# Order of work on VectorE and ScalarE at the end of layer 0 of a two-layer decoder trunk

## The chip, the cores and the metric

The kernel runs on one core of a Trainium2 chip. The metric is the device time of one execution in microseconds (us), the median of three runs. The engines are named as in the profile: PE is TensorE (matmuls; PEld its weight loads), DVE is VectorE, ACT is ScalarE, POOL is GpSimd, and SP issues the loads of weights. Each engine works through its own list of instructions in order; semaphores tie the lists together.

## What is computed

Two layers over 256 tokens of width 1024. Layer 0 mixes tokens by multi-head latent attention, layer 1 by causal attention in blocks with a relative bias from a table; each is followed by an MLP with squared ReLU. Cut to what matters here:

```python
def sq_relu_mlp(h, w_in, w_out):
    a = jax.nn.relu(h @ w_in)
    return (a * a) @ w_out

for i in range(DEPTH):                     # DEPTH = 2
    h = rms_norm(x, attn_norm[i])
    if i % 2 == 0:
        x = x + mla_mixer(h, ...)
    else:
        qkv = (h @ w_qkv).reshape(B, S, 3, 8, 128)
        q, k = rms_norm(qkv[:, :, 0], q_norm), rms_norm(qkv[:, :, 1], k_norm)
        ...                                # logits + table[t5_bucket(pos_q - pos_k)], causal, softmax, @ v, @ w_o
    h = rms_norm(x, mlp_norm[i])
    x = x + sq_relu_mlp(h, w_in, w_out)
```

All of it is float32.

## The kernel before

**Layout.** x is held transposed, as eight column tiles `x[:, d]` of 128 features by 256 tokens. A normed input h is not divided by its root mean square where it is made: h is x times the gain, and the factor of each token (`scale`, or `r3` in layer 1) is applied to the product.

**Three matmuls for one.** To keep float32 accuracy every operand is split in a high part, rounded to fp32r, and a low part, the rest. A product takes three matmuls (`mm3`): high x high, low x high, high x low. For h the parts are hTh (made on ACT) and hTl (made on DVE from x and hTh). For weights they are wh (a cast on ACT, L169) and wl (a subtraction on DVE, L178).

**Weights.** All weights are a list of units of 128x1024 (512 KB). SP loads a unit into one of four `raw` buffers, `hi` casts it, `lo` subtracts, and both results stand in rings of seven. The load of a unit can start when the `lo` of the unit four places ahead of it is done, since that frees its buffer. `hi` goes no further than seven units beyond the last that PE is done with. `both()` issues one `hi` and one `lo`; `fill()` issues `lo` and then `hi`; both do nothing where the ring is full. In what follows **w0, w1, w2 ...** are the units of `w_qkv` in layer 1, in the order in which PE needs them: w0 to w3 for the projection k0, w4 to w7 for q0, w8 to w11 for v0.

**The end of layer 0.** The second matmul of the MLP goes over the eight column tiles d = 0 to 7, in two rounds r; in the last round (r = 1) tile d is finished on the other engines, one after the other:

- `both()` in the middle of the tile's matmuls and `both()` at its end (in d = 6 these split w2 and w3, in d = 7 w4 and w5);
- what `run_fillers` has for this place: in d = 1, 3, 5 and 7 six additions of 0.3 us each that put a block of the relative bias into SBUF (`BiasBlock.add`, L1034); for d = 6 there is nothing;
- `t`: the product times `scale` (DVE, L976);
- `finish0`: x = t + x (L1041; on POOL, for d = 7 on DVE), hTh on ACT (L609), `fill()`, hTl on DVE (L611); for odd d also the square of two tiles of x on ACT (L299), which POOL adds to the sum of squares (L301; after the last tile L306).

The order of all this is the order in which the code issues it (`manual_schedule`); nothing is moved by a scheduler.

**The start of layer 1.** PE goes on with k0 at once: for each column k = 0 to 7 it needs hTh and hTl of that column as the stationary operand and wh and wl of unit w(k // 2) as the moving one; two token tiles of three matmuls each. Then comes q0 for the first token tile (24 matmuls, column k with unit w(4 + k // 2)), four small matmuls for the token sums, q0 for the second token tile, and the transposes of the normed k0 (L372). The norm of k0 is made of squares on ACT (L342), sums over them on DVE (L343), the token sums that DVE copies from PSUM (L316), roots on POOL (L270) and products on DVE (L352).

Of the kernel before, what the change touches and what calls it, by code (L numbers as in the profile page):

```python
# [25 lines left out]
KD = D // P  # L26
# [26 lines left out]
NR = 2  # L53
NPAIR = DFF // (2 * P * NR)
# [6 lines left out]
def trunk(ctx: ExitStack, tc: tile.TileContext, A, out):  # L61
# [9 lines left out]
    def ps():  # L71
        return psum.tile([P, 512], F32, name="ps", tag="ps")

    def room(pool, name):
        if ROOM[name]:
            pool.tile([P, ROOM[name] // 4], F32, name="room_" + name)

    def t2(*shape):
        return work.tile([P, *shape], F32, name="t2", tag="t2")

    def f32(ap):
        return ap.bitcast(F32)
# [4 lines left out]
    def mm3(o, a, b, start, stop, wide=None, between=None):  # L87

        for i, (w, t) in enumerate(((0, 0), (1, 0), (0, 1))):
            if wide and i == 0:  # L90
                mm(wide[0], a[w], wide[1], start, False)
            else:
                mm(o, a[w], b[t], start and i == 0, stop and i == 2)
            if between and between[0] == i:
                between[1]()
# [7 lines left out]
    def wider(bank, b):  # L103
        moved[0] = True
        return bank[:, :S + 2], flat(b[:, :2])[:, :S + 2]
# [55 lines left out]
    def hi(n=1, eng=nc.scalar):  # L161

        for _ in range(n):
            i = len(his)
            if i < min(used[0] + RING, len(units)):
                load_raw()
                w = units[i][1]
                his.append(wsp.tile([P, 1024], F32R, name="wh", tag="wh"))
                (eng.copy if eng is nc.scalar else eng.tensor_copy)(his[i][:, :w], raws[i][:, :w])  # L169

    def lo(n=1, eng=nc.vector):

        for _ in range(n):
            i = len(los)
            if i < len(his):
                w = units[i][1]
                los.append(wsp.tile([P, 1024], F32R, name="wl", tag="wl"))
                eng.tensor_sub(los[i][:, :w], raws[i][:, :w], f32(his[i][:, :w]))  # L178
                load_raw()

    def fill(n=1):
        lo(n)
        hi(n)

    def both(n=1):

        for _ in range(n):
            hi()
            lo()

    def unit(i):
        while len(his) <= i:
            hi()
        while len(los) <= i:
            lo()
        return his[i], los[i]

    def done(i):

        used[0] = max(used[0], i + 1)  # L200

    def part(u, sl):
        return u[0][:, sl], u[1][:, sl]
# [59 lines left out]
    def gain(name, i=0):  # L263
        return gains[:, GOFF[name][0] + i:GOFF[name][0] + i + 1]
# [18 lines left out]
    def hT(k, sl=slice(None)):  # L283
        return hTh[:, k, sl], hTl[:, k, sl]
# [323 lines left out]
    def make_h_filled(k, gname):  # L608
        nc.scalar.activation(hTh[:, k], x[:, k], AF.Copy, scale=gain(gname, k))  # L609
        fill()  # L610
        nc.vector.scalar_tensor_tensor(hTl[:, k], x[:, k], gain(gname, k), f32(hTh[:, k]),  # L611
                                       op0=OP.mult, op1=OP.subtract)
# [267 lines left out]
    for i in range(2):  # L880
        r = slice(i * PE_D, (i + 1) * PE_D)
# [16 lines left out]
    def mlp(l, base, fillers, inside, finish):  # L898

        with tc.tile_pool(name=f"mlp{l}", bufs=1) as pool:  # L900
            scale = pool.tile([P, S], F32, name="scale")
            room(pool, f"a{l}")
            a = [pool.tile([P, 2 * NPAIR, S], F32R, name=f"a{i}") for i in range(2)]
            sums = SumSquares()

            def run_fillers(r, j):
                for g in fillers:
                    if g[0] == (r, j):
                        g[1]()

            def first(b, r, j, split_k, between=None):
                u = [unit(b + 2 * j + i) for i in range(2)]
                p = [ps() for _ in range(2 if split_k else 1)]
                o = [p[f][:, :S] if split_k else p[0][:, f * S:(f + 1) * S] for f in range(2)]
                for f, k in [(f, k) for k in range(KD) for f in range(2)] if split_k else \
                        [(f, k) for f in range(2) for k in range(KD)]:
                    c = (k % 4) * 256 + f * P
                    wide = None
                    if k == f == 0 and not moved[0]:
                        wide = wider(p[f], hTh)  # L920
                    mm3(o[f], part(u[k // 4], slice(c, c + P)), hT(k), k == 0, k == KD - 1, wide,
                        between if (f, k) == (1, KD - 2) else None)
                done(b + 2 * j + 1)


                beside = not split_k and j < NPAIR - 1
                for f, n in ((0, 1), (1, 1)) if split_k else ((0, 2),):
                    src = o[f] if split_k else p[0]
                    rl = t2(n * S)
                    nc.scalar.activation(rl, src, AF.Relu)  # L930
                    sq = t2(n * S)
                    nc.vector.scalar_tensor_tensor(sq, src, 0.0, rl, op0=OP.max, op1=OP.mult)  # L932
                    if l == 1 and r == NR - 1:
                        sq3 = sq.rearrange("p (a b) -> p a b", b=S)
                        nc.vector.tensor_mul(sq3, sq3, scale[:, None, :].to_broadcast([P, n, S]))
                    if beside:
                        both()
                    ah, al = (i[:, 2 * j + f:2 * j + f + n].rearrange("p a b -> p (a b)") for i in a)
                    nc.scalar.copy(ah, sq)
                    nc.vector.tensor_sub(al, sq, f32(ah))  # L940
                both((1 if beside else 2) + (1 <= j < 4))
                run_fillers(r, j)

            for r in range(NR):
                b = base + r * (2 * NPAIR + 2 * KD)
                for j in range(NPAIR):
                    between = inside.get((r, j))
                    if r == 0 and j == 6:
                        pb = ps()
                        between = other_type(1, lambda: mm(pb[:, :S], ones, s, True, True))  # L950
                    first(b, r, j, r == 0 and j == 0, between)
                    if r == 0 and 1 <= j < 5:
                        sums.add(j - 1)
                    if r == 0 and j == 5:
                        s = sums.total()
                    if r == 0 and j == NPAIR - 1:
                        nc.vector.tensor_scalar(scale, pb[:, :S], 1.0 / D, EPS, op0=OP.mult, op1=OP.add)
                        nc.vector.reciprocal(scale, scale)
                b += 2 * NPAIR
                for d in range(KD):  # L960
                    bank = ps()
                    o = bank[:, :S]
                    for f in range(2 * NPAIR):
                        u = unit(b + 2 * d + f // 8)
                        c = (f % 8) * P
                        mm3(o, part(u, slice(c, c + P)), (a[0][:, f], a[1][:, f]), f == 0, f == 2 * NPAIR - 1,
                            wider(bank, a[0]) if f == 0 and not moved[0] else None,
                            inside.get((r, NPAIR + d)) if f == 2 * NPAIR - 2 else None)
                        if f == 7:
                            both()  # L970
                            done(b + 2 * d)
                    both()
                    run_fillers(r, NPAIR + d)
                    if l == 0 or r < NR - 1:
                        y = t2(S)
                        nc.vector.tensor_tensor(y, o, scale, op=OP.mult)  # L976
                        if r < NR - 1:
                            nc.gpsimd.tensor_add(x[:, d], y, x[:, d])  # L978
                            o = None
                        else:  # L980
                            o = y
                    if o is not None:
                        finish(d, o)
                    done(b + 2 * d + 1)


# [52 lines left out]
    def finish0(d, o):  # L1039
        eng = nc.vector if d == KD - 1 else nc.gpsimd  # L1040
        eng.tensor_add(x[:, d], o, x[:, d])  # L1041
        make_h_filled(d, "attn1")
        if d == 0:
            sums1[0] = SumSquares()
        if d % 2:
            sums1[0].add(d // 2)
# [167 lines left out]
```

## Time and profile before

| | |
|---|---|
| three runs | 564.36, 564.68, 564.85 us (median 564.68) |
| the profiled execution, its own time | 564.54 us |
| its span, first to last instruction | 562.7 us |
| granted TensorE clock, mean over the span | 0.997 |
| DMA queues of the weights | 54% of the 16 engines' span |

The page gives the busy time of each engine over the span, then groups of instructions: line, engine, operation, the tile written and the tiles read, count, busy time, mean length. A line such as L85 is that of a helper (`mm`), so PE's work is told apart by the names of the tiles. An answer in order of time has start, length (both in us), engine, line, operation, tiles and, in brackets, how long the engine was idle before and what ended it. Matmuls overlap: each is given 0.39 us at 512 columns though one starts every 0.23 us. A table by stretches gives, for each engine, busy time and number of instructions, and at the end the clock that TensorE was granted (1.00 is full speed), the share of the DMA engines and GB/s.

### The profile page before, as it was taken

Reading aid. Unit: us, or ns where it says so; the run is one execution under the profiler, and the core shown is the slowest. Engines: PE = TensorE matmul, PEld = TensorE weight load, DVE = VectorE, ACT = ScalarE, POOL = GpSimd, SP = SyncE. Lnnn points to the kernel's source line nnn. Section 1 sums busy time; section 2 is a strip of 40 time slices with the busy share of each in tenths; the row PEclk is TensorE's granted clock in tenths of the full one; section 3 lists DMA queues with packets and bytes.
Section 4 is the critical chain, followed back from the end, with each engine's and each line's share of the span. In section 5 each row is a group of like instructions: output and inputs, shape, how many; then the busy total and the mean of one; then the engine's idle time right before and its main releaser. Section 6 shows DMA issues by size and latency. Waiting matters only on the chain.

```text
span 562.7 us, 10806 instructions
## 1 busy us (share of the span) xinstructions
PE 554.5 (99%) x4346; PEld 527.3 (94%) x4346; DVE 396.4 (70%) x654; ACT 302.8 (54%) x495; POOL 94.6 (17%) x105
## 2 busy tenths in 40 slices
PE   8999999999999999999989999999999999999997
PEld 6878999999999999999868888999999999999997
DVE  5997777778987598766678466676876753877630
ACT  6989675665433356343455556646765332655420
POOL 4892100040232000011124100000130211000100
PEclk9999999999999999999989999999999999999999
DMA  8833444686675366544454553453775764575810
GB/s 299 296 123 118 146 139 158 187 280 190 188 223 189 112 217 196 176 155 157 152 182 123 186 191 115 147 181 113 230 224 181 251 201 150 159 219 185 265 45 29
DMA packets 29186, 99.57 MB, mean 177 GB/s; under 512 B 3824, under 2 KB 4720, under 8 KB 29136
## 3 DMA queue, kind: packets, MB, share of 16 engines
q1 hardware_dynamic: 28656, 97.94, 54.1%
q0 software_dynamic: 336, 0.92, 0.4%
q8 instruction: 34, 0.56, 0.4%
q14 instruction: 16, 0.13, 0.1%
q10 hardware_dynamic: 144, 0.02, 0.0%
HBM read 97.82 MB, written 1.05 MB: 176 GB/s over the span
## 4 chain that ended last, share of the span: by engine, by line
PE 95%; DVE 2%; DMA 1%; SPq 1%; issue 1%; POOL 0%; ACT 0%; DVEq 0%
PE ps L85 92%; PE ps L372 1%; PE ps L596 1%; DMA rowp<-in_rowp 1%; DVE wl L178 1%; SPq L158 0%; SPq L230 0%; DVE bias L1034 0%; POOL ang L393 0%; DVE hTl L280 0%; PE ps L512 0%; ACT wh L169 0%; POOL posf L391 0%; ACT hTh L609 0%; DVE x L1041 0%
## 5 line engine op out<-in xcount | busy, mean ns | idle before, releaser
L178 DVE TENSOR_TENSOR wl<-raw,wh 128x1024 fp32r<-128x1024 f32 x177 | 217.0, 1241 | 37.6 <-ACT wh L169 37.0
L169 ACT CAST wh<-raw 128x1024 fp32r<-128x1024 f32 x177 | 182.7, 1047 | 72.2 <-PE ps L85 53.6
L85 PE MATMUL ps<-a,wh 128*128 128x256 f32 x1024 | 175.3, 276 | 0.0
L85 PEld LDWEIGHTS ps<-a,wh 128*128 128x128 f32 x1024 | 154.4, 188 | 0.0
L85 PE MATMUL ps<-a,wl 128*128 128x256 f32 x512 | 142.1, 277 | 0.0
L85 PE MATMUL ps<-hTl,wh 128*128 128x256 f32 x512 | 141.7, 277 | 0.0
L85 PE MATMUL ps<-hTh,wl 128*128 128x256 f32 x512 | 141.7, 277 | 0.0
L85 PE MATMUL ps<-hTh,wh 128*128 128x256 f32 x512 | 141.3, 276 | 0.0
L85 PEld LDWEIGHTS ps<-hTl,wh 128*128 128x128 f32 x512 | 96.1, 188 | 0.1
L85 PEld LDWEIGHTS ps<-hTh,wh 128*128 128x128 f32 x512 | 96.1, 188 | 0.1
L85 PEld LDWEIGHTS ps<-a,wl 128*128 128x128 f32 x512 | 96.1, 188 | 0.0
L85 PEld LDWEIGHTS ps<-hTh,wl 128*128 128x128 f32 x512 | 96.1, 188 | 0.0
L930 ACT ACTIVATE t<-ps 128x512 f32<-128x512 f32 (+1 forms) x34 | 19.5, 572 | 67.5 <-PE ps L85 67.5
L85 PE MATMUL ps<-wh,hTh 128*128 128x512 f32 (+2 forms) x128 | 46.9, 392 | 3.7 <-ACT hTh L609 2.4
L85 PE MATMUL ps<-aT,wh 128*128 128x256 f32 (+1 forms) x256 | 50.4, 288 | 0.0
L932 DVE SCALAR_TENSOR_TENSOR t<-ps,t 128x512 f32<-128x512 f32 (+1 forms) x34 | 22.4, 659 | 38.4 <-ACT t L930 38.0
L85 PE MATMUL ps<-wl,hTh 128*128 128x512 f32 (+2 forms) x128 | 45.9, 384 | 0.2 <-DVE wl L178 0.2
L85 PE MATMUL ps<-wh,hTl 128*128 128x512 f32 (+2 forms) x128 | 45.7, 383 | 0.0
L85 PEld LDWEIGHTS ps<-aT,wh 128*128 128x128 f32 x256 | 40.3, 188 | 0.2
L609 ACT ACTIVATE hTh<-x,gains 128x256 fp32r<-128x256 f32 x24 | 12.2, 510 | 47.9 <-POOL x L1041 29.7
L85 PE MATMUL ps<-aT,wl 128*128 128x256 f32 x128 | 35.6, 278 | 0.0
L978 POOL TENSOR_TENSOR x<-t,x 128x256 f32<-128x256 f32 x16 | 19.4, 1211 | 93.4 <-DVE t L976 93.4
(166 smaller groups left out, 634.7 us busy)
## 6 DMA issues: line engine op xcount, KB each, us to landing
raw<-in_w_in_mlp SPq DMA_DIRECT2D x64, 512.0 KB, 4.1
raw<-in_w_out_mlp SPq DMA_DIRECT2D x64, 512.0 KB, 4.3
raw<-in_w_qkv SPq DMA_DIRECT2D x24, 512.0 KB, 4.2
raw<-in_w_u SPq DMA_DIRECT2D x8, 512.0 KB, 5.9
win<-in_w_in SPq DMA_DIRECT2D x8, 352.0 KB, 5.3
raw<-in_w_o0a SPq DMA_DIRECT2D x4, 512.0 KB, 3.6
raw<-in_w_o0b SPq DMA_DIRECT2D x4, 512.0 KB, 3.6
raw<-in_w_o1a SPq DMA_DIRECT2D x4, 512.0 KB, 3.8
```

The lines of the kernel that those rows point to most:

```text
L85: nc.tensor.matmul(o, a, b, start=start, stop=stop)
L169: (eng.copy if eng is nc.scalar else eng.tensor_copy)(his[i][:, :w], raws[i][:, :w])
L178: eng.tensor_sub(los[i][:, :w], raws[i][:, :w], f32(his[i][:, :w]))
L372: nc.tensor.transpose(pt[:, i * P:(i + 1) * P], yf[:, i * P:(i + 1) * P], ident)
L596: nc.tensor.transpose(pt[:, i * P:(i + 1) * P], self.p[:, i * P:(i + 1) * P], ident)
L609: nc.scalar.activation(hTh[:, k], x[:, k], AF.Copy, scale=gain(gname, k))
L930: nc.scalar.activation(rl, src, AF.Relu)
L932: nc.vector.scalar_tensor_tensor(sq, src, 0.0, rl, op0=OP.max, op1=OP.mult)
L978: nc.gpsimd.tensor_add(x[:, d], y, x[:, d])
```

## The change

In layer 0's last round, for d = 6 and d = 7, the second `both()` and `run_fillers` are issued behind `t` and `finish0` and not ahead of them. For these two tiles `finish0` makes h with `make_h` (L279 and L280 after the change), which issues hTh and hTl with no `fill()` in between; a `fill()` stands behind the moved `both()` instead. All other tiles, rounds and layer 1's MLP are as they were.

```diff
@@ in mlp(), the loop over the column tiles d @@
                         if f == 7:
                             both()
                             done(b + 2 * d)
-                    both()
-                    run_fillers(r, NPAIR + d)
+
+                    last = l == 0 and r == NR - 1 and d >= KD - 2
+                    if not last:
+                        both()
+                        run_fillers(r, NPAIR + d)
                     if l == 0 or r < NR - 1:
                         y = t2(S)
                         nc.vector.tensor_tensor(y, o, scale, op=OP.mult)
...
                     if o is not None:
                         finish(d, o)
+                    if last:
+                        both()
+                        fill()
+                        run_fillers(r, NPAIR + d)
                     done(b + 2 * d + 1)
@@ finish0 @@
         eng = nc.vector if d == KD - 1 else nc.gpsimd
         eng.tensor_add(x[:, d], o, x[:, d])
-        make_h_filled(d, "attn1")
+        (make_h_filled if d < KD - 2 else make_h)(d, "attn1")
```

Lines behind the edit move by three in `mlp` and by seven below it: L976 becomes L979, L1034 becomes L1041, L1041 becomes L1048.

DVE's list before, from the split of w3 (wl_3613) to hTl of column 7. The splits of w4 and w5 are wl_3649 and wl_3689; the two t are those of columns 6 and 7:

```order
L178 TENSOR_TENSOR wl_3613<-raw_3462,wh_3611 128x1024
L976 TENSOR_TENSOR t2_3617<-ps_3556,scale_1319 128x256
L611 SCALAR_TENSOR_TENSOR hTl_155<-x_81,gains_82,hTh_154 128x256
L178 TENSOR_TENSOR wl_3649<-raw_3500,wh_3647 128x1024
L178 TENSOR_TENSOR wl_3689<-raw_3540,wh_3687 128x1024
L1034 TENSOR_TENSOR bias_1312<-ps_3672,mask_146 128x8x16
L1034 TENSOR_TENSOR bias_1312<-ps_3672,bias_1312 128x8x16 x2
L1034 TENSOR_TENSOR bias_1312<-ps_3673,mask_146 128x8x16
L1034 TENSOR_TENSOR bias_1312<-ps_3673,bias_1312 128x8x16 x2
L976 TENSOR_TENSOR t2_3699<-ps_3622,scale_1319 128x256
L1041 TENSOR_TENSOR x_81<-t2_3699,x_81 128x256
L611 SCALAR_TENSOR_TENSOR hTl_155<-x_81,gains_82,hTh_154 128x256
```

The same place of the changed kernel, where w3's split is wl_3618 and w5's wl_3697:

```order
L979 TENSOR_TENSOR t2_3611<-ps_3556,scale_1319 128x256
L280 SCALAR_TENSOR_TENSOR hTl_155<-x_81,gains_82,hTh_154 128x256
L178 TENSOR_TENSOR wl_3618<-raw_3462,wh_3616 128x1024
L178 TENSOR_TENSOR wl_3649<-raw_3500,wh_3647 128x1024
L979 TENSOR_TENSOR t2_3687<-ps_3622,scale_1319 128x256
L1048 TENSOR_TENSOR x_81<-t2_3687,x_81 128x256
L280 SCALAR_TENSOR_TENSOR hTl_155<-x_81,gains_82,hTh_154 128x256
L178 TENSOR_TENSOR wl_3697<-raw_3540,wh_3695 128x1024
L1041 TENSOR_TENSOR bias_1312<-ps_3672,mask_146 128x8x16
L1041 TENSOR_TENSOR bias_1312<-ps_3672,bias_1312 128x8x16 x2
L1041 TENSOR_TENSOR bias_1312<-ps_3673,mask_146 128x8x16
L1041 TENSOR_TENSOR bias_1312<-ps_3673,bias_1312 128x8x16 x2
```

Ahead of both pieces stands the split of w2, behind both that of w6. In column 6 the split of w3 has moved behind t and hTl; in column 7 the split of w5 and the six additions have, so that they now stand directly ahead of the split of w6.

ACT's list before, from the cast of w2 to that of w6 (wh_3734), with hTh of columns 6 and 7 and the square in between:

```order
L169 CAST wh_3581<-raw_3432 128x1024
L169 CAST wh_3611<-raw_3462 128x1024
L609 ACTIVATE hTh_154<-x_81,gains_82 128x256
L169 CAST wh_3647<-raw_3500 128x1024
L169 CAST wh_3687<-raw_3540 128x1024
L609 ACTIVATE hTh_154<-x_81,gains_82 128x256
L299 ACTIVATE t2_3704<-x_81 128x512
L169 CAST wh_3734<-raw_3585 128x1024
```

And in the changed kernel:

```order
L169 CAST wh_3581<-raw_3432 128x1024
L279 ACTIVATE hTh_154<-x_81,gains_82 128x256
L169 CAST wh_3616<-raw_3462 128x1024
L169 CAST wh_3647<-raw_3500 128x1024
L279 ACTIVATE hTh_154<-x_81,gains_82 128x256
L299 ACTIVATE t2_3692<-x_81 128x512
L169 CAST wh_3695<-raw_3540 128x1024
L169 CAST wh_3734<-raw_3585 128x1024
```

The casts of w3 and w5 each stand behind the hTh that they stood ahead of. The lists of PE, POOL and SP have the same rows in the same order; a load of SP waits for the split that frees its buffer, so w7's load now follows the later place of w3's split, and w9's that of w5's.

## The prediction

> **What bounds the kernel now.** The page's busy line comes first.
>
> ```profile
> PE 554.5 (99%) x4346; PEld 527.3 (94%) x4346; DVE 396.4 (70%) x654; ACT 302.8 (54%) x495; POOL 94.6 (17%) x105
> ```
>
> TensorE (PE) is the bound: 562.7 us of span hold 554.5 us of matmuls. An edit on DVE and ACT gains only where PE waits for them, or where PE runs slowly as a result. The view of who waited for whom has one wait of PE that stands far ahead of the others:
>
> ```profile
> PE ps L85 <- ACT hTh L609: 2.4, 1, 2.4
> ```
>
> The chain of work that ended last says where. It runs over PE from 79 us on, leaves PE once, at 279 us, and is back at 285.87:
>
> ```profile
> 281.56 1.22 DVE wl L178
> 282.78 0.21 DVE bias L1034
> ...
> 285.31 0.52 ACT hTh L609
> ...
> 285.87 0.50 PE ps L85
> ```
>
> So PE stands until DVE has finished a weight split and the bias additions, and has then made column 7 of x, of which ACT makes hTh. This is the end of layer 0. PE is already in the first projection of layer 1 (k0: eight columns k, six matmuls each, then q0's 24). PE and its weight loads (PEld) in order of time:
>
> ```profile
> 273.55 0.39 PE L85 MATMUL ps<-wh,hTh 128*128 128x512 f32 x1
> 281.94 0.40 PE L85 MATMUL ps<-wh,hTh 128*128 128x512 f32 x1
> 283.11 0.39 PE L85 MATMUL ps<-wl,hTh 128*128 128x512 f32 x1
> 285.87 0.50 PE L85 MATMUL ps<-wh,hTh 128*128 128x512 f32 x1 [2.36 <-ACT hTh L609]
> 290.60 0.40 PE L85 MATMUL ps<-wh,hTh 128*128 128x512 f32 x1
> 282.88 0.19 PEld L85 LDWEIGHTS ps<-wl,hTh 128*128 128x128 f32 x1
> 285.87 0.19 PEld L85 LDWEIGHTS ps<-wh,hTh 128*128 128x128 f32 x1 [2.80 <-ACT hTh L609]
> 286.39 0.19 PEld L85 LDWEIGHTS ps<-wh,hTl 128*128 128x128 f32 x1 [0.34 <-DVE hTl L611]
> ```
>
> Column 0 begins at 273.55 and column 6 at 281.94: 36 matmuls in 8.39 us, 0.233 each. Column 7 was due at 283.11 + 0.233 = 283.35. From 281.94 to 290.60 stand 18 matmuls (6 of column 6, 6 of column 7, 6 of q0), which should take 4.20 us and took 8.66. **4.46 us are lost**, though the wait is called 2.4. The table by stretches shows the rest:
>
> ```profile
> 3.87:7.29 3.42, 2.35 (x13) 1.79 (x12) 1.99 (x5) 2.02 (x4) 0.00 (x0) 1.00 1.01 310
> 7.29:10.70 3.41, 3.41 (x22) 3.10 (x21) 2.51 (x4) 2.49 (x5) 0.73 (x2) 1.00 1.04 391
> 283.77:287.18 3.41, 1.29 (x4) 0.86 (x5) 1.88 (x6) 1.87 (x3) 0.70 (x1) 1.00 0.62 241
> 287.18:290.59 3.41, 3.41 (x9) 2.63 (x8) 3.28 (x3) 3.41 (x6) 2.20 (x2) 0.50 0.22 46
> ```
>
> The first number after the length is PE's busy time; the third from the end is the granted clock. In the 3.41 us behind the stall it is 0.50: some 1.7 us are lost to half speed. PE was busy for 1.29 of 3.41 us just before that. Near the start it was busy for 2.35 of 3.42, and the stretch that followed was at full clock. So a hole of about 1 us has passed here without a price, and one of 2.1 us has not.
>
> The Trainium skill ("TensorE: Matmul & The Clock Gate", section "Why this matters for your kernels") says to avoid idle gaps of PE above some 3 us, since a window of idle brings half clock. The trace has half clock behind a gap of 2.4 us, below that figure. If the page's figure held and this dip had another cause, the dip would stay and the gain would lack 1.7 us; the measurement decides, so I count the dip as part of the stall.
>
> **The change part by part.** No instruction is added or removed; DVE, ACT and the loads that follow DVE's splits move. The old schedule on DVE (all of its pieces that matter), then ACT and POOL:
>
> ```profile
> 275.06 1.56 DVE L178 TENSOR_TENSOR wl<-raw,wh 128x1024 fp32r<-128x1024 f32 x1 [0.97 <-ACT wh L169]
> 277.67 0.41 DVE L976 TENSOR_TENSOR t<-ps,scale 128x256 f32<-128x256 f32 x1
> 279.48 0.48 DVE L611 SCALAR_TENSOR_TENSOR hTl<-x,gains,hTh 128x256 fp32r<-128x256 f32 x1 [1.40 <-ACT hTh L609]
> 280.42 2.36 DVE L178 TENSOR_TENSOR wl<-raw,wh 128x1024 fp32r<-128x1024 f32 x2 [0.46 <-ACT wh L169]
> 282.70 0.28 DVE L1034 TENSOR_TENSOR bias<-ps,mask 128x128 f32<-128x128 f32 x1
> 284.40 0.41 DVE L976 TENSOR_TENSOR t<-ps,scale 128x256 f32<-128x256 f32 x1
> 284.85 0.43 DVE L1041 TENSOR_TENSOR x<-t,x 128x256 f32<-128x256 f32 x1
> 285.85 0.48 DVE L611 SCALAR_TENSOR_TENSOR hTl<-x,gains,hTh 128x256 fp32r<-128x256 f32 x1 [0.58 <-ACT hTh L609]
> 276.54 1.21 DVE L178 TENSOR_TENSOR wl<-raw,wh 128x1024 fp32r<-128x1024 f32 x1
> 287.31 1.55 DVE L178 TENSOR_TENSOR wl<-raw,wh 128x1024 fp32r<-128x1024 f32 x1 [0.97 <-ACT wh L169]
> 288.78 1.75 DVE L178 TENSOR_TENSOR wl<-raw,wh 128x1024 fp32r<-128x1024 f32 x1
> 285.31 0.51 ACT L609 ACTIVATE hTh<-x,gains 128x256 fp32r<-128x256 f32 x1 [3.96 <-DVE x L1041]
> 286.24 1.03 ACT L169 CAST wh<-raw 128x1024 fp32r<-128x1024 f32 x1
> 292.42 1.06 ACT L169 CAST wh<-raw 128x1024 fp32r<-128x1024 f32 x1 [1.33 <-DMA raw<-in_w_qkv]
> 286.48 1.30 POOL L301 TENSOR_TENSOR ssum<-ssum,t 128x512 f32<-128x512 f32 x1 [7.58 <-ACT t L299]
> 287.86 1.60 POOL L306 TENSOR_TENSOR ssum<-ssum 128x256 f32<-128x256 f32 x1
> ```
>
> Column 6. Its t (277.67) loses the split of w3 ahead of it and starts at 276.54, where that split began: 1.13 us earlier. The steps up to hTl (x on POOL, hTh on ACT) keep their distances, and so do the casts and splits behind them: the pair at 280.42 starts at 279.29. It now holds w3 and w4.
>
> Column 7. In the old order t followed the pair after 2.28 us of splits and 1.70 us of bias additions (282.70 to 284.40). The additions now stand behind, so t starts at 279.29 + 2.28 = 281.57, **2.83 us earlier** (1.13 + 1.70). hTh then runs from 282.48 to 282.99, hTl from 283.02 to 283.50.
>
> What PE needs: a weight load starts with the matmul ahead of it (both rows at 282.88), so hTh was due at 283.11 and was waited for until 285.87, 2.76 us. 2.83 just covers it. hTl was loaded at 286.39 instead of 283.35: 3.04 us late, of which 0.2 stay. As the start of its load overlaps the matmul ahead, I take **0.15 us** (bounds 0 and 0.4, should a link of the chain be 0.2 slower). w3's split ends at about 280.5, before column 6 needs it at 281.94 and later: no cost.
>
> What is late next. The additions and w5's split have moved ahead of w6's split, and PE, being earlier, wants w6 earlier. ACT casts w5 behind hTh and the square of column 7, at 282.48 + (286.24 - 285.31) = 283.41; the split follows 1.07 later (287.31 - 286.24), at 284.48. Beside POOL's sums (286.48 and 287.86, now 2.83 earlier) a split took 1.55 to 1.75 us, otherwise 1.21; I take 1.55. The additions then run from about 285.95 to 287.65, and w6's split to 288.9. PE wants that part in the third matmul of q0's column 4, the 21st from 283.35 on: 283.35 + 20 x 0.233 + 0.15 = 288.16. **New wait 0.9 us**: the 0.77 of this sum, and some for additions beside POOL, which the trace does not show. Bounds: 0.4 with a split of 1.21, 1.3 with one of 1.75 and 0.3 on the additions. PE then stands for under 1.1 us, less than the hole that passed at full clock. w7's split ends at 290.0; PE wants it at 290.4.
>
> Loads. Each load waits until the split four units ahead of it frees its buffer. w9's load now waits for w5's split, which ends at about 286.0 instead of 282.78. Rows 287.31 and 292.42 show such a load: 288.86 to 292.42, 3.56 us. So ACT can cast w9 only at 289.6, and its squares of k0's norm, queued behind, start at 290.6. The norm's reductions on DVE then end at about 292.5. What follows is bound to this:
>
> ```profile
> 295.35 0.16 DVE L316 COPY ss<-ps 128x2 f32<-128x2 f32 x1 [2.48 <-PE ps L85]
> 300.09 0.75 DVE L352 SCALAR_TENSOR_TENSOR t<-ps,rs,hrs 128x512 f32<-128x512 f32 x1 [0.20 <-POOL hrs L270]
> 301.02 0.87 PE ps L372 x8
> ```
>
> The copy at 295.35 can run at 292.5, 2.85 earlier. The second k0 row product (300.09 to 300.84) had some 0.4 us to spare before the transposes of its tile, the last four of the eight. PE arrives there 4.46 - 0.15 - 0.9 = 3.4 earlier, the product 2.85: 3.4 - 2.85 - 0.4 = **0.15 us** (bounds 0, and 0.6 with a load of 4.0). After that PE has no wait left in this trace, and the work is the same.
>
> Sum: 4.46 - 0.15 - 0.9 - 0.15 = **3.26 us**. The profiled run took 564.54 (562.7 of span and 1.84 around it), 0.14 below the median of 564.68; 564.68 - 3.26 gives **561.4**. With the bounds, the forecast's own range is 560.5 to 562.4.
>
> **The rivals.**
>
> 1. Nothing waits anew: the split is uncontended, PE is a little late, and w6 is there. Then 4.1 to 4.4 us are gained: 560.3 to 560.6. Against it: even the lower bound of w6's wait is 0.4.
> 2. The half clock stays or comes again behind the new wait. Price 1.7 us: 563.1. For it: half clock was granted once for a hole of 2.1 us, and the limit lies anywhere between 1.1 and 2.1. By the figure of the Trainium skill cited above the old gap was too short to be the cause, and the dip would stay.
> 3. Column 7 comes late after all: POOL's x or a cast takes longer in its new neighbourhood, and up to 1 us of the old wait remains: 561.9 to 562.6.
> 4. The gain is eaten in layer 1. If w9's load takes longer than the 3.56 us counted, ACT, the norm and PE's transposes each move by as much. At 2.1 us more (5.7) the gain is under 0.2%, 1.1 us, which is about what a measurement here can tell from no change: 563.6 to 565.8.
> 5. Slower: the same load at over 7.9 us, 4.4 us more than counted; with 5 us more it gives 566.4. The page's median for these loads is 4.2 us:
>
> ```profile
> raw<-in_w_qkv SPq DMA_DIRECT2D x24, 512.0 KB, 4.2
> ```
>
> That makes the fourth unlikely and the fifth more so; they also stand for a wait that I have overlooked.
>
> **How the numbers follow.** Forecast 0.63, rivals in order 0.10, 0.08, 0.08, 0.07, 0.04. Time 561.4. The range runs from 560.1 (all of the 4.46 and a little scatter) to 563.2 (rival 2), which leaves out the last two and some edges. Faster by over 0.2%: the forecast and the first three hold 0.89, less 0.02 for their upper edges, 0.87; within it 0.07 and these edges, 0.09; slower 0.04.
>
> **What the profile after would show.** PE's wait for hTh gone from the list, or below 0.3; a wait of PE for a wl of about 0.9 at 288 us; granted clock 1.00 in every stretch from 280 to 295; column 7's t on DVE at about 281.6, additions from 286; the transposes of k0 at about 297.8 instead of 301.02. Half clock at 287 to 292, a wait at the transposes above 0.6, or column 7's t after 282 would each prove a step wrong.

## The result, and the profile after

The changed kernel took 561.45 us (median of six executions, 560.99 to 562.01) where the kernel before took 564.76 beside it (median of six, 562.97 to 576.66; the highest stands far from the others and is left out of the ratio). The ratio is 0.9948, 95% interval 0.9933 to 0.9963: about half a per cent faster. The forecast was 561.4. A second set of executions of the same two kernels gave 561.41 and 564.39, ratio 0.9954 (0.9938 to 0.9969). The profiled execution took 561.53, its span is 559.8.

From the page of the changed kernel, the busy line and the row of the granted clock in 40 slices:

```profile
PE 553.9 (99%) x4346; PEld 527.7 (94%) x4346; DVE 395.5 (71%) x654; ACT 302.9 (54%) x495; POOL 93.8 (17%) x105
PEclk9999999999999999999999999999999999999999
```

The work is the same, and no slice is below full clock. Who waited for whom (line, what was waited for, us in total, times, longest), PE's longest rows:

```profile
PE ps L85 <- DVE warm L218: 1.0, 1, 1.0
PE ps L85 <- DVE wh L446: 0.7, 1, 0.7
PE ps L85 <- DVE wl L178: 0.7, 1, 0.7
```

The 2.4 us for hTh are gone; a wait of 0.7 for a split (wl), at 289.11, is new. PE and PEld of the changed kernel in order of time, at the places that the prediction named:

```profile
273.74 0.39 PE L85 MATMUL ps<-wh,hTh 128*128 128x512 f32 x1
283.53 0.40 PE L85 MATMUL ps<-wh,hTh 128*128 128x512 f32 x1
289.11 0.50 PE L85 MATMUL ps<-wl,hTh 128*128 128x512 f32 x1 [0.65 <-DVE wl L178]
297.60 1.34 PE L372 MATMUL ps<-ident,t 128*128 128x128 f32 x8
298.69 0.48 PE L85 MATMUL ps<-wh,hTh 128*128 128x512 f32 x1
283.75 0.19 PEld L85 LDWEIGHTS ps<-wh,hTl 128*128 128x128 f32 x1 [0.27 <-DVE hTl L280]
289.11 0.19 PEld L85 LDWEIGHTS ps<-wl,hTh 128*128 128x128 f32 x1 [1.09 <-DVE wl L178]
298.27 0.42 PEld L372 LDWEIGHTS ps<-ident,t 128*128 128x128 f32 x4 [0.32 <-PE ps L372]
```

k0 starts at 273.74 (0.19 later than in the trace of before, which is scatter from earlier in the program, so the table below counts from there). Column 7 follows column 6 without a gap. Three small stops remain: hTl at 283.75, the first part of w6 at 289.11, and the second half of the transposes at 298.27. The table by stretches (PE's busy time follows the length, the granted clock is third from the end):

```profile
280.36:283.77 3.41, 3.41 (x17) 2.55 (x15) 2.73 (x5) 1.13 (x4) 0.00 (x0) 1.00 0.42 154
283.77:287.18 3.41, 3.41 (x16) 2.76 (x16) 2.44 (x5) 3.24 (x4) 2.90 (x2) 1.00 0.40 159
287.18:290.59 3.41, 2.76 (x12) 1.94 (x11) 3.34 (x6) 1.27 (x2) 0.00 (x0) 1.00 0.61 177
```

The stretch that ran at 0.50 before has 1.00. DVE and ACT of the changed kernel around the moved pieces:

```profile
275.26 1.55 DVE L178 TENSOR_TENSOR wl<-raw,wh 128x1024 fp32r<-128x1024 f32 x1 [0.97 <-ACT wh L169]
276.74 0.41 DVE L979 TENSOR_TENSOR t<-ps,scale 128x256 f32<-128x256 f32 x1
279.48 2.36 DVE L178 TENSOR_TENSOR wl<-raw,wh 128x1024 fp32r<-128x1024 f32 x2 [0.45 <-ACT wh L169]
281.76 0.42 DVE L979 TENSOR_TENSOR t<-ps,scale 128x256 f32<-128x256 f32 x1
283.22 0.48 DVE L280 SCALAR_TENSOR_TENSOR hTl<-x,gains,hTh 128x256 fp32r<-128x256 f32 x1 [0.58 <-ACT hTh L279]
284.67 1.55 DVE L178 TENSOR_TENSOR wl<-raw,wh 128x1024 fp32r<-128x1024 f32 x1 [0.97 <-ACT wh L169]
286.14 0.28 DVE L1041 TENSOR_TENSOR bias<-ps,mask 128x128 f32<-128x128 f32 x1
287.84 3.49 DVE L178 TENSOR_TENSOR wl<-raw,wh 128x1024 fp32r<-128x1024 f32 x3
291.48 1.28 DVE L343 TENSOR_REDUCE hss<-t 128x4 f32<-128x512 f32 x2 [0.15 <-ACT t L342]
292.67 0.15 DVE L316 COPY ss<-ps 128x2 f32<-128x2 f32 x1
289.90 1.05 ACT L169 CAST wh<-raw 128x1024 fp32r<-128x1024 f32 x1 [2.14 <-DMA raw<-in_w_qkv]
290.86 1.07 ACT L342 ACTIVATE t<-ps 128x512 f32<-128x512 f32 x2
```

DVE has each row where the prediction put it, shifted by the 0.19. The next table takes the starts of PE's first matmul of k0, of column 7, of the 21st matmul counted from there (which wants w6's low part), of the transposes and of v0, and the end of the span, all in us from k0's start:

| kernel | column 7 | w6's part | transposes | v0 | end of span |
|---|---|---|---|---|---|
| before | 12.31 | 18.92 | 27.30 | 28.09 | 289.18 |
| the change | 9.79 | 15.38 | 23.86 | 24.95 | 286.02 |

The change is 2.52 ahead at column 7 and 3.54 at w6's part. There the half clock is gone and the new wait has been paid. It gives back 0.10 on the way to the transposes and 0.30 in them, and behind v0 nothing changes any more: 3.16 at the end of the span.

### The profile page after: what moved, and what is told of

It reads as the page before. It is cut to its first block, busy times and chain, and to the rows that moved or that the text cites. A ratio compares the mean times of both kernels' runs of the same rounds, so it can differ in the third digit from the quotient of the medians.

```text
span 559.8 us, 10805 instructions
## 1 busy us (share of the span) xinstructions
PE 553.9 (99%) x4346; PEld 527.7 (94%) x4346; DVE 395.5 (71%) x654; ACT 302.9 (54%) x495; POOL 93.8 (17%) x105
## 4 chain that ended last, share of the span: by engine, by line
PE 90%; DVE 4%; issue 2%; ACT 2%; POOL 1%; DMA 1%; SPq 0%; ACTq 0%; POOLq 0%; DVEq 0%
PE ps L85 87%; DVE wl L178 2%; PE ps L372 2%; ACT wh L169 1%; DVE bias L1041 1%; PE ps L596 1%; POOL x L1048 1%; DMA win<-in_w_in 1%; ACT t L299 0%; DVE t L979 0%; DVE st L1024 0%; PE ps L512 0%; DVE x L1048 0%; DVE t L1057 0%; SPq L230 0%
## 5 line engine op out<-in xcount | busy, mean ns | idle before, releaser
L270 POOL TENSOR_TENSOR hrs<-hss,mhalf 128x4 f32<-128x4 f32 (+1 forms) x18 | 23.2, 1299 | 65.2 <-DVE hss L347 48.6
```

What stands on the lines that cost most here:

```text
L270: nc.gpsimd.tensor_tensor(dst, t, mhalf[:, :n].rearrange("p (a b) -> p a b", b=t.shape[-1]) if len(t.shape) == 3 else mhalf[:, :n], op=OP.pow)
```

## The experiments

Two theories stood against each other on the first question, which part of the edit brings column 7 forward. A is the prediction's: 1.13 us by column 6's part and 1.70 by the additions. B: column 6's part brings nothing, since w3's split, once behind column 6, stands ahead of column 7, and the 1.13 belong to w5's split. The diffs are against the changed kernel unless another is named. Medians are of 4 to 10 executions unless a single execution is named; the ratio is the one against the kernel before of the same set, with its 95% interval.

### Which part of the edit

**The change for column 7 alone.**

```diff
-                    last = l == 0 and r == NR - 1 and d >= KD - 2
+                    last = l == 0 and r == NR - 1 and d == KD - 1
...
-        (make_h_filled if d < KD - 2 else make_h)(d, "attn1")
+        (make_h_filled if d < KD - 1 else make_h)(d, "attn1")
```

> Only column 7 is reordered; column 6 is as before. Theory A, the prediction's own sum: column 7's t is 2.83 us earlier by 1.13 (column 6's edit) and 1.70 (the additions). Without the first, hTh comes 2.76 - 1.70 = 1.1 us late and hTl 1.3: PE waits for them, about 562.6. Theory B: column 6's edit only lets w3's split change places with t, so the split is still ahead of column 7; what brings column 7 forward is that its own w5 split (1.14) and the additions (1.70) stand behind. Then this kernel is like the full change: column 7's t at about 281.6 us, no wait for hTh, a wait of 0.7 to 0.9 for w6's split, 561.4.

Measured: 561.64 us, ratio 0.9957 (0.9942 to 0.9973), the time of the full change. k0 starts at 273.98. DVE in order of time, one split and then t of column 7:

```profile
280.84 1.23 DVE L178 TENSOR_TENSOR wl<-raw,wh 128x1024 fp32r<-128x1024 f32 x1 [0.46 <-ACT wh L169]
281.99 0.42 DVE L979 TENSOR_TENSOR t<-ps,scale 128x256 f32<-128x256 f32 x1
```

t stands 8.01 behind k0's start, and in the full change 281.76 - 273.74 = 8.02. Without column 6's part, column 7 is as early as with it. Theory A falls.

**The change for column 6 alone.**

```diff
-                    last = l == 0 and r == NR - 1 and d >= KD - 2
+                    last = l == 0 and r == NR - 1 and d == KD - 2
...
-        (make_h_filled if d < KD - 2 else make_h)(d, "attn1")
+        (make_h_filled if d != KD - 2 else make_h)(d, "attn1")
```

> Only column 6 is reordered; column 7 is as before. Theory A: column 7 is 1.13 us earlier; PE's wait for hTh falls from 2.4 to about 1.3, and the time to 562.0 to 563.6, by whether the half clock stays. Theory B: the split of w3 that column 6 no longer waits for stands ahead of column 7 instead, so column 7's t stays at 284.4, the wait at 2.4, the half clock behind it, and the time at that of the kernel before (0.998 to 1.002).

Measured: 563.97 us, ratio 0.9999 (0.9984 to 1.0013): nothing. DVE in order of time, then PE's wait from the view of waits:

```profile
279.89 3.49 DVE L178 TENSOR_TENSOR wl<-raw,wh 128x1024 fp32r<-128x1024 f32 x3 [0.45 <-ACT wh L169]
285.00 0.42 DVE L979 TENSOR_TENSOR t<-ps,scale 128x256 f32<-128x256 f32 x1
```

```profile
PE ps L85 <- ACT hTh L609: 2.4, 1, 2.4
```

Three splits (w3, w4, w5) now stand ahead of column 7's t, where there were two, and PE waits its 2.4 us as before. Column 6's part only moves one split from ahead of one t to ahead of the next. B holds.

**The additions alone behind column 7's h; both splits stay ahead.**

```diff
-                    last = l == 0 and r == NR - 1 and d >= KD - 2
+                    last = l == 0 and r == NR - 1 and d == KD - 1
+                    both()
                     if not last:
-                        both()
                         run_fillers(r, NPAIR + d)
...
                     if last:
-                        both()
-                        fill()
                         run_fillers(r, NPAIR + d)
...
-        (make_h_filled if d < KD - 2 else make_h)(d, "attn1")
+        make_h_filled(d, "attn1")
```

> Only the six bias additions of the last place move behind column 7's h; both splits of columns 6 and 7 stay ahead. Theory B (column 7 is brought forward by 1.14 from its own w5 split and 1.70 from the additions): t at about 282.7 us where the kernel before has 284.4, so hTh is 1.06 and hTl 1.34 late and PE loses about 1.2; the hole is too short for half clock (every run at a mean clock of 1.00); w5's split is where it was, so w9's load and the norm are not delayed and w6's split is in time. 561.4 to 561.8, like the full change by another way. Rival (a hole of over 1 us brings half clock too): 563.

Measured: 561.50 us, ratio 0.996 (0.9947 to 0.9973), the gain of the full change. From k0's start column 7 comes at 10.63, w6's part at 15.69, the transposes at 24.07 and v0 at 24.87. Waits and PEld:

```profile
PE ps L85 <- ACT hTh L609: 0.7, 1, 0.7
```

```profile
284.69 0.19 PEld L85 LDWEIGHTS ps<-wh,hTh 128*128 128x128 f32 x1 [1.11 <-ACT hTh L609]
```

PE now waits 0.84 for column 7 (10.63 against 9.79). hTl is late as well and costs another 0.3: w6's part comes 15.69 - 10.63 = 5.06 behind column 7, and 4.77 in the run with late additions below, where PE hardly waits at either place. So w6's split, which has one split less ahead of it, costs nothing here. At w6's part this kernel is 0.31 behind the change. It makes that up in the transposes, which take 0.80 instead of 1.09: w5's split is early, so the norm is not late. In time, the additions alone bring all that the change brings.

**w5's split alone behind column 7's h; the additions stay ahead.**

```diff
                     if not last:
                         both()
-                        run_fillers(r, NPAIR + d)
+                    run_fillers(r, NPAIR + d)
...
                         fill()
-                        run_fillers(r, NPAIR + d)
```

with `last` and `make_h` for column 7 only, as in the first experiment.

> Only the split of w5 (and its cast) moves behind column 7's h; the bias additions stay ahead of it. Theory B: t at about 283.3, 1.14 earlier; hTh 1.6 and hTl 1.9 late, PE loses 1.8. If half clock follows a hole by its place in windows of 3.41 us that run free of the program, a hole of this length is too short to fill over half of any window, and all runs are at a mean clock of 1.00: 562.0 to 562.4. If a hole of 1.6 is enough in some places, the runs fall into two groups 1.5 us apart, as those of the kernel before do.

Measured: 563.32 us, ratio 0.9994 (0.9984 to 1.0005): not to be told from before, and slower than I expected. Its waits, PEld at the stall, a stretch of its table, and DVE's reductions of k0's norm:

```profile
PE ps L85 <- ACT hTh L279: 1.2, 1, 1.2
PE ps L85 <- DVE warm L218: 1.0, 1, 1.0
PE ps L372 <- DVE t L352: 0.8, 2, 0.5
```

```profile
284.25 0.19 PEld L85 LDWEIGHTS ps<-wh,hTh 128*128 128x128 f32 x1 [1.68 <-ACT hTh L279]
```

```profile
281.41:284.83 3.42, 2.15 (x9) 1.19 (x7) 2.59 (x8) 1.14 (x3) 0.00 (x0) 1.00 0.48 153
284.83:288.24 3.41, 3.41 (x15) 2.78 (x16) 2.55 (x2) 3.41 (x4) 2.91 (x2) 1.00 0.00 0
```

```profile
292.42 1.28 DVE L343 TENSOR_REDUCE hss<-t 128x4 f32<-128x512 f32 x2 [1.22 <-ACT t L342]
```

Column 7 did about as expected: w6's part comes at 16.25 from k0's start, 1.69 behind the 14.56 of the run with late additions below, which hardly waits there (1.8 were forecast). What I had left out is the norm. w5's split ends late, so w9's load, its cast, the squares of k0 behind it on ACT and the reductions are late (DVE is idle for 1.22 us, waiting for the squares), and the transposes wait 0.8. The clock stays at 1.00 although PE was busy for only 2.15 of 3.42 us in the stretch of the stall.

### What holds the gain at 3.2

**The additions behind the splits of w5 to w8.**

```diff
                         fill()
-                        run_fillers(r, NPAIR + d)
...
             done(Q0 + k // 2)
+    blocks[-1].add()
     total = sums1[0].total()
```

> The full change, but the last six bias additions are issued behind the splits of w6, w7 and w8 instead of ahead of them. Theory A: the wait for w6's split is the last loss; it goes (split done at 287.4, wanted at 288.2), and the time falls by 0.8 to 560.6. Theory B: the norm of k0 caps it. Its reductions cannot start before about 291.4, since ACT's squares stand behind the cast of w9, whose load waited for w5's split; so PE arrives 0.9 earlier at the transposes and waits there for 0.9 to 1.2 instead of 0.3, and the time stays at 561.4 (ratio to the full change 0.999 to 1.001).

Measured: 561.91 us, ratio 0.9965 (0.9951 to 0.9979), no better than the change. w6's wait is gone (its part comes at 14.56 from k0's start, 0.82 earlier), and the view of waits has another at the head:

```profile
PE ps L372 <- DVE t L352: 1.1, 2, 0.7
```

The transposes start at 23.84, as in the change (23.86), and v0 at 25.25, 0.30 later. The norm of k0 sets this time: a wait ahead of it that is taken away comes back there. But it is not w9's load alone that holds the norm in this kernel. DVE comes to the reductions without a pause:

```profile
291.83 1.27 DVE L343 TENSOR_REDUCE hss<-t 128x4 f32<-128x512 f32 x2
```

Directly ahead of this row stand the six additions, which the edit has moved there. ACT's squares start at 290.80, as in the change (290.86), and would have let the reductions start some 0.4 earlier, at about 291.4 (an estimate: in the change they start 0.62 behind the squares). So w9's load would have held the norm almost as late; the last 0.4 is the additions' own. The next kernel takes both out of the norm's way.

**The norm early.** The additions go behind k0's reductions, w9's cast and w8's split behind the squares:

```diff
         if k % 2:
-            fill()
+            if k < KD - 1:
+                fill()
...
         post1("k0", t, False)
+    blocks[-1].add()
...
     root1("k0", 1)
-    fill(2)
+    fill()
```

with `run_fillers` taken out at column 7 as in the experiment before.

> The additions behind the reductions of k0's norm, and the cast of w9 and the split of w8 behind the squares of k0, so that the norm no longer stands behind w9's load. If the cap of the norm is as described (theory B of the run with late additions): squares at 287.7 instead of 290.9 us, the copy of the token sums at 291.4 instead of 292.7, no wait for w6 and at most 0.3 at the transposes or the following splits: 560.2 to 560.6, less than the full change. If the norm is not the cap, this gives the same as the run with late additions.

Measured: 568.73 us, ratio 1.0085 (1.0066 to 1.0103): slower by 7 us than the change, against my expectation. At this place it does what it should: v0 starts at 24.16 instead of 24.95. The loss is elsewhere, in layer 1's MLP. The next kernels are made to find it.

**The same with one cast more behind the roots**, and with column 6 as before the change:

```diff
-    fill(2)
+    fill()
+    hi()
```

> As the run with the norm made early, but with column 7 alone reordered and w10's cast issued in time, so that no split in the heads of layer 1 is late. If the slow last MLP of the run before (a matmul of 256 columns every 118 ns from 370 us on, where the other kernels have 113) came from the late splits and PE's wait at 361 us, it goes, and the earlier norm shows its own gain: 560.3 to 560.8. If the pace depends on something else that the early norm sets, the MLP stays at 118 and the time at 567 to 568.

Measured: 561.02 us, ratio 0.9956 (0.9939 to 0.9973). That is above the range that I expected. v0 starts at 24.12, 0.83 ahead of the change, and the span ends at 285.56, 0.46 ahead: some 0.4 is lost again behind v0, and no run here shows to what. DVE in order of time and the wait that is left:

```profile
288.98 1.27 DVE L343 TENSOR_REDUCE hss<-t 128x4 f32<-128x512 f32 x2
```

```profile
PE ps L372 <- DVE t L352: 0.2, 1, 0.2
```

The reductions come 2.5 earlier than in the change. It ran again, in one set with the change:

> The changed kernel again, to be timed beside the best variant: 561.0 to 561.9, every run at a mean clock of 0.999 or 1.00.

> The variant with column 7 alone reordered, the norm early and all casts in time, timed beside the changed kernel: 0.4 to 0.6 us below it, 560.9 to 561.2.

The change took 561.41 (0.9954, 0.9938 to 0.9969) and this variant 561.50 (0.9954, 0.9939 to 0.9969). From k0's start to the end of the span it is again shorter, 285.58 against 285.93, but k0's start scattered from 273.1 to 274.3 over the traces, and in whole times the two cannot be told apart, where I had expected 0.4 to 0.6 us. So I claim no better version.

**That variant without the additional cast** (the diff is against that variant), **and the early norm with both columns changed and the cast** (the same line added to the kernel of 568.73):

```diff
     fill()
-    hi()
```

> The run with the early norm and all casts in time, less one thing: w10's cast is issued one place later again, as in the slow kernel. If late splits in the heads of layer 1 set the slow pace of the last MLP, a split is late again near 361 us, PE waits there, the matmuls after 370 us come every 118 ns, and the time is 567 to 569. If the pace came from the reordering of column 6, which this kernel does not have, the matmuls come every 113 ns and the time is about 561.3.

> The slow kernel (early norm, columns 6 and 7 reordered) plus the one thing that it lacked, w10's cast one place earlier. If late splits set the pace, it is at 113 ns and about 561.0 to 561.3; if the reordering of column 6 together with the early norm does, it stays at 118 and 568 to 569.

A single execution each: 568.76 without the cast (561.02 with it), 561.33 with both columns and the cast (568.73 without it). So the 7 us hang on one cast (with the split that follows it) being issued a place later, and not on column 6.

**The change with a single late split**, far from the edit: one `fill()` in layer 1's heads is left out (`mid` is None in layer 0 alone), and a later one does its work.

```diff
         o(0)
-        fill()
+        if mid is None:
+            fill()
         turn("q1", 0)
```

> The changed kernel with one fill left out in the heads of layer 1 (behind the first head's share of the output projection), so that every later split comes one place later; the norm is as in the changed kernel. If a late split and PE's short wait for it inside the output projection set the slow pace of the last MLP, PE waits for a wl near 361 us, matmuls come every 118 ns from 370 on, and the time is 567 to 569. If the early norm is needed for the slow pace, they come every 113 ns, and the time is 561.5 to 562.5.

A single execution: 569.16 us. Its v0 starts at 24.93, as in the change. The stretch from 420 to 450 us, in layer 1's MLP, first of the change, then of this kernel, and this kernel's only wait of PEld between 358 and 364 us:

```profile
420.00:450.00 30.00, 30.00 (x267) 30.00 (x266) 21.07 (x22) 14.45 (x16) 3.86 (x4) 1.00 0.67 211
```

```profile
420.00:450.00 30.00, 30.00 (x255) 29.95 (x255) 20.16 (x22) 13.37 (x15) 3.14 (x3) 1.00 0.65 202
```

```profile
361.41 0.19 PEld L85 LDWEIGHTS ps<-aT,wl 128*128 128x128 f32 x1 [0.31 <-DVE wl L178]
```

PE is busy throughout and at full clock in both, but the 30 us hold 267 matmuls in the one and 255 in the other. That is where the 7 us are, and one late split in the heads brings it about as well; the early norm is not needed for it.

The late split does not begin the slow pace, though. The rows of the output projection, ahead of the MLP, show where the two kernels part. One matmul in three has wl. Here are two such rows nine matmuls apart, two more behind them, and the one matmul of 258 columns that the code puts between the pairs (`wider`, at column tile 5 of the output projection). First the change, then this kernel:

```profile
372.32 0.28 PE L85 MATMUL ps<-aT,wl 128*128 128x256 f32 x1
373.38 0.28 PE L85 MATMUL ps<-aT,wl 128*128 128x256 f32 x1
374.08 0.28 PE L85 MATMUL ps<-aT,wl 128*128 128x256 f32 x1
375.10 0.28 PE L85 MATMUL ps<-aT,wl 128*128 128x256 f32 x1
L85 PE MATMUL ps<-aT,wh 128*128 128x258 f32 x1 | 0.3, 280 | 0.0
```

```profile
372.83 0.28 PE L85 MATMUL ps<-aT,wl 128*128 128x256 f32 x1
373.89 0.28 PE L85 MATMUL ps<-aT,wl 128*128 128x256 f32 x1
374.61 0.28 PE L85 MATMUL ps<-aT,wl 128*128 128x256 f32 x1
375.67 0.28 PE L85 MATMUL ps<-aT,wl 128*128 128x256 f32 x1
L85 PE MATMUL ps<-aT,wh 128*128 128x258 f32 x1 | 0.3, 281 | 0.0
```

In the change nine matmuls take 1.06 us ahead of the wide one and 1.02 behind it, 118 and 113 ns each. In this kernel they take 1.06 on both sides. All fourteen traces have the slow pace in the output projection; eleven leave it at the wide matmul, and the three slow kernels do not. So what goes along with the late split is that the wide matmul no longer ends the slow pace.

## Why the prediction was right, and where it was not

- **What bounds.** Right. The gain is PE's stall behind column 7 and its consequences; behind v0 the two traces run alike (261.09 and 261.07 us to the end).
- **Column 7's 2.83 us.** The size was right: t was forecast at 281.57, with k0's 0.19 at 281.76, and there it is. The attribution was wrong. The prediction wrote of column 6: "Its t (277.67) loses the split of w3 ahead of it and starts at 276.54, where that split began: 1.13 us earlier", and passed these 1.13 on to column 7. Column 6's part alone gives nothing, and the change without it gives all. What fails is the step that passes column 6's gain on: "the pair at 280.42 starts at 279.29. It now holds w3 and w4". The pair is there in the changed kernel (279.48), but it is a pair only because w5's split has left; with column 6 as before, w4's split stands there alone, at 280.84, and t starts as early from k0's start (8.01 against 8.02). The split that column 7 loses is its own. That the size came out right all the same is luck: the splits of w3 and w5 are equally long (1.21 and 1.22), which hid the mistake.
- **hTl, 0.15.** The load at 283.75 had waited 0.27; the next matmuls ran some 0.1 late.
- **The new wait for w6, 0.9.** Right: 15.38 - 14.56 = 0.82. (The sum that the prediction gives as 0.77 is 288.9 - 288.16 = 0.74 by its own figures.) But it does not cost 0.82 by itself. With it removed, the transposes started where they did: the norm was held by the additions now ahead of it, and without them w9's load would have held it to within 0.4 of that.
- **The loads and the norm.** w9's cast was forecast at 289.6, the squares at 290.6, the copy at 292.5, and came at 289.90, 290.86 and 292.67, again with the 0.19.
- **The transposes, 0.15.** Undersized: they took 298.69 - 297.60 = 1.09 where they had taken 0.79 before, so 0.30, inside the bounds. (The range of 560.5 to 562.4 is counted from the profiled 564.54; from the median, which the 561.4 is counted from, it is 0.14 higher.)
- **The half clock, 1.7.** Right for the profiled execution and the medians, wrong as a certainty. Over the sets of the experiments, 27 of 47 executions of the kernel before had a mean clock of 0.997, as in its profile, and 20 had 1.000; the first took 563.83 to 565.21 us (median 564.7), the others 562.59 to 563.91 (median 563.1). So the same stall cost some 1.6 us more in the one group than in the other. Against the second the change gains 1.7 and against the first 3.3. That the measured gain is so near the forecast 3.26 is in part chance: four of the five executions of before that count in the result took 564.4 to 565.2, like the first group. No execution of the changed kernel (12), of column 7 alone (5) or of the additions alone (9) was below 0.999, and none of the ten with w5's split alone, whose weight loads stood for 1.7 us at the stall. That kernel is as fast as the kernel before without its dip, 563.3 against 563.1: it cuts the stall, pays it back at the norm, and saves only the dip.

Rival 2 kept the half clock for a shorter wait, and none came. The Trainium skill ("TensorE: Matmul & The Clock Gate", section "Why this matters for your kernels") would have had the dip stay, since it puts the limit for an idle gap at some 3 us. The runs do not agree: with the 2.4 us gone the dip is gone in every execution. What the same page says under "What's actually happening" fits the runs: the window in which activity is judged runs freely, so that the cost depends on where in it an event falls. One stall gave two groups of times 1.6 us apart. And the window at half clock lies at another place of the program in the kernel with column 6 alone:

```profile
286.31:289.72 3.41, 3.25 (x8) 2.44 (x8) 2.30 (x3) 3.41 (x6) 2.56 (x2) 0.50 0.19 78
```

It begins 12.19 us behind k0's start (274.12), and in the trace of before 13.63, though column 7 comes at 12.35 and 12.31. No trace of an execution with this stall and without the dip was kept.

Rivals 1 and 3 to 5 did not occur. Rival 1, that nothing waits anew, had the norm against it as much as w6: the kernels with w6's part in time and the norm early gained at most 0.46 us more from k0's start.

## What to carry to other kernels

When an edit moves an instruction from ahead of one step to behind it, ask which step it now stands ahead of: on an engine with a list in order, only what passes the last waited-for step is gained. Behind a stall that is removed, follow the next two deadlines and not one, with loads that a freed buffer starts among them; here weight split and norm were late by nearly the same, so taking away one brought nothing. Look at several executions' granted clocks before a clock dip is counted in full, and let a change far from the end be judged by the whole span, since it can change the pace of matmuls elsewhere.

## What the runs showed of the hardware

- **A stall has two prices.** The stall of 2.4 us took the mean clock to 0.997 in 27 of 47 executions of the kernel before and in 5 of 10 with column 6 alone, and left it at 1.000 in the others; the medians of before's two groups lie 1.6 us apart. A stall of 1.2 us, with 1.7 of the weight loads, never did in ten.
- **PE has two paces at full clock.** In the output projection of layer 1 a 256-column matmul starts every 118 ns in all fourteen traces. In eleven of them it starts every 113 ns from one matmul of 258 columns on (between 373.38 and 374.08 in the change) and through the MLP. Both paces stand at a granted clock of 1.00, with no wait of PE within the stretch from 420 to 450 us. In the three slow kernels (568.73, 568.76 and 569.16 us) the same wide matmul changes nothing. Each of these has a wait of 0.31 us for a split near 361 us, inside the stretch that is slow in all; none of the eleven has it. The order of PE's matmuls is the same in the change and in the kernel with the single late split. How the late split keeps the wide matmul from ending the slow pace stays open, and no run moves the wide matmul or leaves it out.
